# Seven block products for two pairs of gate-and-up chunks a layer, the rest of gate and up in row form, weights in rings

## The chip, the core and the metric

One core of a Trainium2 chip runs the whole program. It has a tensor engine (PE: matrix products and transposes), VectorE (DVE), ScalarE (ACT), GpSimd (POOL) and a queue for transfers on SyncE (SP); every engine works through its own list of instructions in order, and semaphores hold an instruction until what it needs is there. The metric is the device time of the program in microseconds (us).

## What is computed

A trunk of four layers on 256 tokens of width 1024. Each layer has a mixer (layers 0 and 3 banded attention, layer 1 gated linear attention, layer 2 differential attention), a residual with layer norm, then a SwiGLU feed-forward part of hidden width 2816, and again a residual with layer norm:

```python
def swiglu(x, w_gate_up, w_down):
    g, u = jnp.split(x @ w_gate_up, 2, axis=-1)
    return (jax.nn.silu(g) * u) @ w_down

for i in range(DEPTH):
    y = mixer_i(h)
    h = layer_norm(DN_ALPHA * h + y, ln1_g[i], ln1_b[i])
    h = layer_norm(DN_ALPHA * h + swiglu(h, ffn_w_gate_up[i], ffn_w_down[i]), ln2_g[i], ln2_b[i])
```

All inputs are float32. The change touches `x @ w_gate_up` above all: [256 x 1024] by [1024 x 5632] in each layer.

## The kernel before

**Precision.** A float32 value is kept as two float32r parts, high and low (high is the value rounded, low the rest), and a product is made of three matmuls: high with low, high with high, low with high.

**Weights.** They are laid out in DRAM in chunks of 512 columns; a gate-and-up chunk holds 256 columns of the gate and the 256 of the up projection that belong to them, so a layer has 11 such chunks. `w_tiles` (L101) loads two k-tiles of a chunk (512 KB, SP's queue, L109), writes the high part on ACT (L110) and the low part on DVE (L111). There are `RAWB` = 6 buffers for loads and `WB` = 8 for each of the split parts; 4 KB a partition each.

**Two forms of product.** `run_rows` (L141) is row form: tokens on the partitions of the result, 512 weight columns a bank; one step is one k-tile for one half of the tokens, three matmuls (L175 to L177). Half 1 of the tokens runs `lag` steps behind half 0, by default `LAG` = 10, so that a weight tile stays in use for that long. `run_cols` (L182) is column form: the weights stand still, 128 columns at a time, and all 256 tokens stream through, high and low side by side (L196, L197); the four tiles of a chunk stay in use until its last column block. A result in row form has to be transposed to be the next product's stationary input (`split_T`, L219: transposes on PE, the split on ACT L211 and DVE L212); one in column form needs no transpose but an addition of its two halves of the bank (L868, L869).

**Order.** The program is written in one order and the framework's scheduler then fixes each engine's list by that order's priority and by readiness. Work that follows from a finished product is put off by a number of steps (`defer`, `tick`).

**The feed-forward part** (`ffn`, L843): the first two chunks of gate and up in row form (while the second half of the norm is still under way), chunks 2 to 10 in column form, then the down projection in row form, 22 k-tiles by two chunks with the default lag. Row form: ACT takes the silu of the gate (L855), DVE multiplies (L857), and `split_T` turns the result. Scale and shift of the coming norm are loaded by `late_load` (L119) from POOL's queue, each as one [128 x 1024] tile, after POOL has read one column of something just written (L122).

**The norm** (`Norm`, L254) adds the residual on DVE (L276), takes statistics (L287, L300), makes the inverse deviation on POOL (L245, L249), scales and shifts on DVE (L307, L319), and turns the result into the next stage's input `xT`.

**The mixers** run their value (or gate) chunks in row form, the query and key chunks in column form with scores and softmax put in between, and the output projection in row form (`out_proj`).

Of the kernel before, what the change touches and what calls it, by code (L numbers as in the profile page):

```python
# [29 lines left out]
D_SCORES, D_TURN, D_TURN_DIFF, D_VALUES, D_VALUES_DIFF, D_OUT = 4, 7, 6, 3, 2, 6  # L30
D_GATE2, D_GATE3, D_STATE, D_READ, D_GLA_OUT = 3, 8, 2, 4, (6, 5)
D_NORM, D_HIDDEN = 8, 4


@with_exitstack
def trunk_kernel(
# [30 lines left out]
    wp = ctx.enter_context(tc.tile_pool(name="wp", bufs=1))  # L67
    act = ctx.enter_context(tc.tile_pool(name="act", bufs=1))
# [7 lines left out]

    def slab(shape, dtype=F32):
        return act.tile(shape, dtype, tag="slab", bufs=4, name=nm("slab"))

    def k3(shape, dtype=F32):  # L80
        return act.tile(shape, dtype, tag="k3", bufs=5, name=nm("k3"))

    def k2(shape, dtype=F32):
        return act.tile(shape, dtype, tag="k2", bufs=8, name=nm("k2"))

    def k1(shape, dtype=F32):
        return act.tile(shape, dtype, tag="k1", bufs=6, name=nm("k1"))
# [923 lines left out]
```

## Time and profile before

| | us |
|---|---|
| time before, median of 3 runs | 1211.81 (1207.75 to 1213.13) |
| span of the profiled execution | 1209.5 |
| PE busy | 1191.5 (99%) |
| DVE busy | 829.6 (69%) |
| ACT busy | 665.5 (55%) |
| POOL busy | 97.7 (8%) |
| granted TensorE clock, mean of the span | 0.998 of 2.4 GHz |

The profile is of one execution; its span is 2.3 us under the median. PE's share counts the matmuls' modelled ends, which overlap, so the pace is read from the starts of successive matmuls. The gate-and-up stage of layer 0 lies from 123.6 to 248.25 us, its down projection from 248.25 on; the column-form part of layer 1 lies from 441.73 to 541.83.

### The profile page before, as it was taken

The numbers are of one execution on the slowest core, as the hardware profiler recorded it, in microseconds if no ns is written. First come the engines' busy times: TensorE is split into PE (matmuls) and PEld (weight loads), VectorE is DVE, ScalarE is ACT, GpSimd is POOL, SyncE is SP. The second block draws the span as 40 slices with busy tenths as digits, with TensorE's granted clock in tenths as the row PEclk, the third lists the DMA queues.
The fourth block names the chain that finished last, engine by engine and source line by source line (L and its number), as shares of the span: only waits on it lengthen the run. The fifth ranks groups of instructions, "written<-read, shape, count | busy, mean of one in ns | idle before, by whom it ended". The sixth has DMA issues, their size and how long they took to land.

```text
span 1209.5 us, 17080 instructions
## 1 busy us (share of the span) xinstructions
PE 1191.5 (99%) x6224; PEld 993.6 (82%) x6224; DVE 829.6 (69%) x1418; ACT 665.5 (55%) x1169; POOL 97.7 (8%) x188
## 2 busy tenths in 40 slices
PE   7999999999999999999999999999999999999997
PEld 5888888888887888888887778888888888888885
DVE  6687866745656777764667787676466888666644
ACT  6566555643664455663446656556344774665531
POOL 0130000000101000000012110000001200000000
PEclk9999999999999999999999999999999999999999
DMA  9654646556464456555564355665557544655641
GB/s 340 225 189 140 210 173 226 175 176 194 155 229 136 137 195 230 193 184 187 189 226 152 122 168 188 225 198 171 188 185 235 188 126 156 205 208 197 205 143 35
DMA packets 62772, 223.88 MB, mean 185 GB/s; under 512 B 7264, under 2 KB 7776, under 8 KB 62688
## 3 DMA queue, kind: packets, MB, share of 16 engines
q1 hardware_dynamic: 58176, 207.64, 52.1%
q0 software_dynamic: 4512, 15.14, 3.5%
q8 instruction: 49, 0.80, 0.3%
q14 instruction: 35, 0.29, 0.1%
HBM read 221.71 MB, written 1.05 MB: 184 GB/s over the span
## 4 chain that ended last, share of the span: by engine, by line
PE 94%; DVE 2%; ACT 2%; DMA 1%; POOL 0%; issue 0%; SPq 0%; POOLq 0%; DVEq 0%; ACTq 0%
PE mm L196 28%; PE mm L175 15%; PE mm L176 15%; PE mm L197 15%; PE mm L177 15%; PE tp L422 2%; PE tp L224 2%; ACT k L445 1%; PE tp L491 1%; DVE k L430 1%; DMA raw<-in_a_qkv_dram 1%; DVE wl L111 0%; PE tp L512 0%; PE tp L514 0%; PE tp L513 0%
## 5 line engine op out<-in xcount | busy, mean ns | idle before, releaser
L111 DVE TENSOR_TENSOR wl<-raw,wh 128x1024 fp32r<-128x1024 f32 (+1 forms) x394 | 476.0, 1214 | 180.6 <-ACT wh L110 177.7
L196 PE MATMUL mm<-slab,wh 128*128 128x512 f32 x1568 | 555.6, 397 | 0.0
L110 ACT CAST wh<-raw 128x1024 fp32r<-128x1024 f32 (+1 forms) x394 | 406.4, 1047 | 196.7 <-PE mm L177 185.2
L197 PE MATMUL mm<-slab,wl 128*128 128x256 f32 x1568 | 440.8, 281 | 0.0
L196 PEld LDWEIGHTS mm<-slab,wh 128*128 128x128 f32 x1568 | 294.3, 188 | 71.1 <-issue 4.6
L175 PE MATMUL mm<-wl,slab 128*128 128x512 f32 x784 | 311.5, 397 | 7.9 <-DVE wl L111 7.9
L177 PE MATMUL mm<-wh,slab 128*128 128x512 f32 x784 | 307.4, 392 | 0.0
L176 PE MATMUL mm<-wh,slab 128*128 128x512 f32 x784 | 307.2, 392 | 0.0
L197 PEld LDWEIGHTS mm<-slab,wl 128*128 128x128 f32 x1568 | 296.5, 189 | 0.7 <-issue 0.3
L175 PEld LDWEIGHTS mm<-wl,slab 128*128 128x128 f32 x784 | 147.8, 189 | 41.1 <-DVE wl L111 8.5
L177 PEld LDWEIGHTS mm<-wh,slab 128*128 128x128 f32 x784 | 147.6, 188 | 31.7 <-DVE slab L212 0.8
L176 PEld LDWEIGHTS mm<-wh,slab 128*128 128x128 f32 x784 | 147.8, 189 | 30.4 <-issue 1.8
L869 DVE TENSOR_TENSOR k<-mm,k 128x256 f32<-128x256 f32 x144 | 60.6, 421 | 82.9 <-ACT k L868 82.9
L868 ACT COPY k<-mm 128x256 f32<-128x256 f32 x144 | 53.7, 373 | 71.4 <-PE mm L197 71.1
L871 ACT ACTIVATE k<-k 128x256 f32<-128x256 f32 x72 | 29.8, 414 | 46.7 <-DVE k L869 46.7
L245 POOL TENSOR_SCALAR sm<-mv 128x1 f32<-128x1 f32 x16 | 14.1, 883 | 500.4 <-DVE mv L300 500.4
L211 ACT CAST slab<-k 128x256 fp32r<-128x256 f32 (+1 forms) x76 | 31.8, 418 | 40.9 <-DVE k L875 37.4
L212 DVE TENSOR_TENSOR slab<-k,slab 128x256 fp32r<-128x256 f32 (+1 forms) x76 | 33.0, 435 | 23.1 <-ACT slab L211 23.1
L445 ACT ACTIVATE k<-k,nmx 128x128 f32<-128x128 f32 x96 | 42.5, 444 | 8.4 <-DVE nmx L441 8.3
L211 ACT CAST slab<-tp 128x512 fp32r<-128x512 f32 (+1 forms) x56 | 27.1, 495 | 26.6 <-PE tp L224 24.5
L430 DVE CUSTOM_DVE_ANT_0 k<-tp,k 128x128 f32<-128x128 f32 x96 | 28.6, 353 | 10.1 <-PE tp L422 9.0
L212 DVE TENSOR_TENSOR slab<-tp,slab 128x512 fp32r<-128x512 f32 (+1 forms) x56 | 30.6, 569 | 4.6 <-ACT slab L211 4.5
(133 smaller groups left out, 669.5 us busy)
## 6 DMA issues: line engine op xcount, KB each, us to landing
raw<-in_w_gu_dram SPq DMA_DIRECT2D x176, 512.0 KB, 4.4
raw<-in_w_down_dram SPq DMA_DIRECT2D x88, 512.0 KB, 4.2
raw<-in_a_qkv_dram SPq DMA_DIRECT2D x46, 512.0 KB, 4.7
raw<-in_b_in_dram SPq DMA_DIRECT2D x24, 512.0 KB, 3.6
raw<-in_c_qkv_dram SPq DMA_DIRECT2D x24, 512.0 KB, 3.6
raw<-in_a_o_dram SPq DMA_DIRECT2D x16, 512.0 KB, 3.9
k<-in_a_bias_dram POOLq DMA_DIRECT2D x16, 256.0 KB, 4.5
lng<-in_ln_g_dram POOLq DMA_DIRECT2D x8, 512.0 KB, 5.7
```

The lines of the kernel that those rows point to most:

```text
L110: nc.scalar.copy(out=wh[:, k, :], in_=raw[:, k, :])
L111: nc.vector.tensor_tensor(out=wl[:, k, :], in0=raw[:, k, :], in1=wh[:, k, :].bitcast(F32), op=ALU.subtract,)
L175: nc.tensor.matmul(b, xh, wl, start=first, stop=False)
L176: nc.tensor.matmul(b, xh, wh, start=False, stop=False)
L177: nc.tensor.matmul(b, xl, wh, start=False, stop=last)
L196: nc.tensor.matmul(b, wh[:, cs], xk, start=kt == 0, stop=False)
L197: nc.tensor.matmul(b[:, :256], wl[:, cs], xk[:, :256], start=False, stop=kt == NKT - 1)
L211: nc.scalar.copy(out=h, in_=val)
L212: nc.vector.tensor_tensor(out=dst[:, ks, slice(256 + cs.start, 256 + cs.stop)], in0=val, in1=h.bitcast(F32), op=ALU.subtract,)
L445: nc.scalar.activation(pr[:, m, SL[t]], pr[:, m, SL[t]], AF.Exp, bias=nmx[:, t, m : m + 1], accum_out=sm[:, t, m : m + 1],)
L868: nc.scalar.copy(out=lo, in_=b[:, 256:])
L869: nc.vector.tensor_tensor(out=lo, in0=b[:, :256], in1=lo, op=ALU.add)
```

## The change

- **Gate and up in row form.** Chunks 0 and 1 stay as they are. Chunks 2 and 3, and chunks 8 and 9, become two pairs; chunks 4 to 7 and 10 run in row form with a lag of 2 (`PLAIN = (4, 1)`).
- **A pair by seven products.** The input is cut into 2 x 2 blocks (token half by even or odd k-tile), the 1024 columns of the pair into 2 x 2 blocks of weights, b11, b12, b21, b22 (four k-tiles by 512 columns; the host lays each out as one block of 8 KB a partition). `run_seven` makes seven products of 4 steps each instead of eight: of plain blocks and of sums and differences of blocks (Winograd's form of Strassen's scheme). t1 = b12 - b11 and t2 = b22 - t1 are made on DVE, t3 = b22 - b12 and t4 = b21 - t2 on POOL, all written over one of their inputs. Each product's weights are split by `halves` in one piece of 2048 columns. The seven results are added up on DVE, out of PSUM, into the four blocks of the result.
- **Sums of the input.** `blocks_of` puts together the float32 input on POOL (2048 columns a partition), makes the four sums s1 to s4 on POOL (512 columns each) and splits them on ACT and DVE, once a layer.
- **Rings.** Loads come from a ring of 36 KB a partition, split parts from a ring of 56 KB, instead of 24 KB and 64 KB of fixed buffers. A tile takes its room when the tiles that lay there before are released.
- **Pools by stage.** Most activations come from a pool that a mixer or a feed-forward part opens and closes. The hidden values are one tile of 22 k-tiles; the next stage's input has a tile of its own; `k1` has 5 buffers for 6, `k2` 10 for 8, `slab` 3 for 4.
- **Scale and shift** of the norms arrive in halves of 512 columns, four loads for two.

The diff, cut to its core (the lines of `Norm`, of the pools and the comments are left out where they only rename):

```diff
-RAWB = 6  # weight loads under way, 2 k-tiles each
-WB = 8  # split weights on chip, 2 k-tiles each
-LAG = 10  # k-tiles that token half 1 runs behind half 0
+RAW = 36 << 10
+SPLIT = 56 << 10
+LAG = 10
+PLAIN = (4, 1)
...
+    raw_ring = wp.ring(RAW, name="raw")
+    split_ring = wp.ring(SPLIT, name="split")
...
+    def in_stage(fn, *args, **kw):
+        with tc.tile_pool(name=nm("stage"), bufs=1, reuse_waits="tile") as pool:
+            stage.append(pool)
+            fn(*args, **kw)
+            stage.pop()
+    def st(shape, dtype, tag, bufs):
+        return stage[-1].tile(shape, dtype, tag=tag, bufs=bufs, name=nm(tag))
...
-        return act.tile(shape, dtype, tag="slab", bufs=4, name=nm("slab"))
+        return st(shape, dtype, "slab", 3)
-        return act.tile(shape, dtype, tag="k2", bufs=8, name=nm("k2"))
+        return st(shape, dtype, "k2", 10)
...
-        raw = wp.tile([P, 2, 512], F32, tag="raw", bufs=RAWB, name=nm("raw"))
-        wh = wp.tile([P, 2, 512], F32R, tag="wh", bufs=WB, name=nm("wh"))
-        wl = wp.tile([P, 2, 512], F32R, tag="wl", bufs=WB, name=nm("wl"))
+        raw = raw_ring.tile([P, 2, 512], F32, name=nm("raw"))
...
+    def halves(w, n):
+        wh = split_ring.tile([P, n, 512], F32R, name=nm("wh"))
+        wl = split_ring.tile([P, n, 512], F32R, name=nm("wl"))
+        nc.scalar.copy(out=wh, in_=w)
+        nc.vector.tensor_tensor(out=wl, in0=w, in1=wh.bitcast(F32), op=ALU.subtract)
+        return [(wh[:, k, :], wl[:, k, :]) for k in range(n)]
...
+                (to, n, ap.partition_broadcast(P)[:, n * 512 : (n + 1) * 512])
+                for to, ap in ((self.g, g_ap), (self.b, b_ap))
+                for n in range(2)
             ]
...
+    def blocks_of(xT):
+        xf = st([P, NKT, 2 * P], F32, "gb", 1)
+        nc.gpsimd.tensor_tensor(
+            out=xf,
+            in0=xT[:, :, : 2 * P].bitcast(F32),
+            in1=xT[:, :, 2 * P :].bitcast(F32),
+            op=ALU.add,
+        )
+        a11, a12, a21, a22 = (
+            xf[:, k::2, t * P : (t + 1) * P] for t in range(2) for k in range(2)
+        )
+        s1, s2, s3, s4 = f = [st([P, 4, P], F32, "u", 4) for _ in range(4)]
+        nc.gpsimd.tensor_tensor(out=s1, in0=a21, in1=a22, op=ALU.add)
+        nc.gpsimd.tensor_tensor(out=s2, in0=s1, in1=a11, op=ALU.subtract)
+        nc.gpsimd.tensor_tensor(out=s3, in0=a11, in1=a21, op=ALU.subtract)
+        nc.gpsimd.tensor_tensor(out=s4, in0=a12, in1=s2, op=ALU.subtract)
+        x = st([P, 2, 4, 4, P], F32R, "sx", 1)
+        for i in range(4):
+            nc.scalar.copy(out=x[:, 0, i], in_=f[i])
+            nc.vector.tensor_tensor(
+                out=x[:, 1, i], in0=f[i], in1=x[:, 0, i].bitcast(F32), op=ALU.subtract
+            )
+        def plain(k, t):
+            ts = [slice(o + t * P, o + (t + 1) * P) for o in (0, 256)]
+            return lambda p: [xT[:, 2 * p + k, c] for c in ts]
+        def diff(i):
+            return lambda p: [x[:, j, i, p] for j in range(2)]
+        return dict(
+            a11=plain(0, 0), a12=plain(1, 0), a22=plain(1, 1),
+            s1=diff(0), s2=diff(1), s3=diff(2), s4=diff(3),
+        )
+    def run_seven(w, x, done):
+        raw = []
+        for i in range(4):
+            r = raw_ring.tile([P, 4, 512], F32, name=nm("raw"))
+            nc.sync.dma_start(r, w[i].rearrange("p (k n) -> p k n", k=4))
+            raw.append(r)
+        b11, b12, b22, b21 = raw
+        def minus(engine, out, in0, in1):
+            engine.tensor_tensor(out=out, in0=in0, in1=in1, op=ALU.subtract)
+            return out
+        def product(a, w):
+            bk = bank("mm")
+            wts = halves(w, 4)
+            for p in range(4):
+                (xh, xl), (wh, wl) = x[a](p), wts[p]
+                nc.tensor.matmul(bk, xh, wl, start=p == 0, stop=False)
+                nc.tensor.matmul(bk, xh, wh, start=False, stop=False)
+                nc.tensor.matmul(bk, xl, wh, start=False, stop=p == 3)
+                tick(1)
+            return bk
+        def u():
+            return st([P, 512], F32, "u", 4)
+        def plus(out, in0, in1):
+            nc.vector.tensor_tensor(out=out, in0=in0, in1=in1, op=ALU.add)
+        p1 = product("a11", b11)
+        s1, u2, u3, c22 = (u() for _ in range(4))
+        nc.scalar.copy(out=s1, in_=p1)
+        t1 = minus(nc.vector, b11, b12, b11)
+        p5 = product("s1", t1)
+        t3 = minus(nc.gpsimd, b12, b22, b12)
+        t2 = minus(nc.vector, t1, b22, t1)
+        p6 = product("s2", t2)
+        plus(u2, p6, s1)
+        t4 = minus(nc.gpsimd, t2, b21, t2)
+        p7 = product("s3", t3)
+        plus(u3, p7, u2)
+        plus(c22, p5, u3)
+        plus(u2, p5, u2)
+        done(1, 1, c22)
+        p2 = product("a12", b21)
+        plus(s1, p2, s1)
+        done(0, 0, s1)
+        p3 = product("s4", b22)
+        plus(u2, p3, u2)
+        done(0, 1, u2)
+        p4 = product("a22", t4)
+        plus(u3, p4, u3)
+        done(1, 0, u3)
...
+        def turn(c, t, hd):
+            split_T(hd, hid, t, 2 * c, 2)
+            if t == 1 and c >= 5:
+                if not gb:
+                    gb.append(st([P, 4, 512], F32, "gb", 1))
+                norm.load(
+                    hid[:, 2 * c, P : P + 1].bitcast(F32),
+                    lambda sh: gb[0][:, 3 - len(norm.loads)],
+                )
+        run_rows([(plain(c), K8, src, gated(c)) for c in range(2)])
+        x = blocks_of(xT)
+        c = 2
+        for n in PLAIN:
+            run_seven(
+                w[c : c + 2].rearrange("c (i p n) -> (c i) p n", i=2, p=P), x, lambda t, j, y, c=c: gated(c + j)(t, y)
+            )
+            c += 2
+            run_rows([(plain(k), K8, src, gated(k)) for k in range(c, c + n)], lag=2)
+            c += n
...
```

## Rows read from the trace of the kernel before

**Rows 1.** The page's head: span, busy time by engine, end chain by engine.

```profile
span 1209.5 us, 17080 instructions
PE 1191.5 (99%) x6224; PEld 993.6 (82%) x6224; DVE 829.6 (69%) x1418; ACT 665.5 (55%) x1169; POOL 97.7 (8%) x188
...
PE 94%; DVE 2%; ACT 2%; DMA 1%; POOL 0%; issue 0%; SPq 0%; POOLq 0%; DVEq 0%; ACTq 0%
```

**Rows 2.** Windows (stretch and length, busy by engine, clock, DMA): rows, columns, columns.

```profile
123.60:146.28 22.68, 22.68 (x108) 18.74 (x107) 19.11 (x27) 12.15 (x17) 2.00 (x2) 1.00 0.62 199
146.28:248.25 101.97, 101.97 (x580) 88.51 (x578) 68.30 (x106) 60.19 (x107) 3.83 (x7) 1.00 0.58 199
...
441.73:541.83 100.10, 100.10 (x580) 88.25 (x578) 68.20 (x106) 60.55 (x107) 3.56 (x6) 1.00 0.60 204
```

**Rows 3.** Timeline (start, duration, engine, line): row-form steps without and with transposes.

```profile
142.40 0.39 PE L177 MATMUL mm<-wh,slab 128*128 128x512 f32 x1
142.64 0.38 PE L224 MATMUL tp<-ident,k 128*128 128x128 f32 x2
...
143.32 0.40 PE L177 MATMUL mm<-wh,slab 128*128 128x512 f32 x1
...
263.27 0.39 PE L175 MATMUL mm<-wl,slab 128*128 128x512 f32 x1
...
263.95 0.39 PE L175 MATMUL mm<-wl,slab 128*128 128x512 f32 x1
```

**Rows 4.** Groups of instructions by form: count, busy us, mean ns, idle before.

```profile
L111 DVE TENSOR_TENSOR wl<-raw,wh 128x1024 fp32r<-128x1024 f32 x390 | 473.2, 1219 | 179.7 <-ACT wh L110 176.8
L110 ACT CAST wh<-raw 128x1024 fp32r<-128x1024 f32 x390 | 403.9, 1051 | 195.5 <-PE mm L177 185.2 <-PE mm L196 3.1 <-DMA raw<-in_a_qkv_dram 1.8
...
L212 DVE TENSOR_TENSOR slab<-tp,slab 128x256 fp32r<-128x256 f32 x24 | 10.0, 418 | 2.0 <-ACT slab L211 1.9
...
L497 DVE TENSOR_TENSOR k<-tp,k 128x512 fp32r<-128x512 f32 x16 | 11.0, 688 | 3.8 <-ACT k L496 3.7
...
L857 DVE TENSOR_TENSOR k<-k,mm 128x256 f32<-128x256 f32 x16 | 6.6, 414 | 0.6
...
L111 DVE TENSOR_TENSOR wl<-raw,wh 128x512 fp32r<-128x512 f32 x4 | 2.7, 692 | 0.9 <-ACT wh L110 0.9
L110 ACT CAST wh<-raw 128x512 fp32r<-128x512 f32 x4 | 2.5, 618 | 1.1 <-DMA raw<-in_a_qkv_dram 1.1
```

**Rows 5.** Transfers by line: count, KB each, median us from issue to landing.

```profile
raw<-in_w_gu_dram SPq DMA_DIRECT2D x176, 512.0 KB, 4.4
```

**Rows 6.** Timeline of POOL: a fill of one column and of 512.

```profile
0.95 0.10 POOL L98 MEMSET powt<- 128x1 f32 x1
...
83.62 0.53 POOL L637 MEMSET k<- 128x512 f32 x1
```

**Rows 7.** Timeline of POOL and DVE: POOL's one-column reads, alone and beside splits.

```profile
71.73 0.18 POOL L122 COPY lng<-slab 128x1 f32<-128x1 f32 x1 [1.99 <-DVE slab L396]
...
117.66 0.18 POOL L245 TENSOR_SCALAR sm<-mv 128x1 f32<-128x1 f32 x1 [27.44 <-DVE mv L300]
...
127.19 1.17 DVE L111 TENSOR_TENSOR wl<-raw,wh 128x1024 fp32r<-128x1024 f32 x1
127.35 1.05 POOL L245 TENSOR_SCALAR sm<-mv 128x1 f32<-128x1 f32 x1 [8.86 <-DVE mv L300]
...
941.53 2.35 DVE L111 TENSOR_TENSOR wl<-raw,wh 128x1024 fp32r<-128x1024 f32 x2
941.68 2.25 POOL L122 COPY k<-slab 128x1 f32<-128x1 f32 x1 [2.69 <-DVE slab L396]
```

**Rows 8.** Timeline of a down projection: a tile's release and its next split.

```profile
263.04 0.39 PE L177 MATMUL mm<-wh,slab 128*128 128x512 f32 x1
...
263.51 1.05 ACT L110 CAST wh<-raw 128x1024 fp32r<-128x1024 f32 x1 [1.67 <-PE mm L177]
...
264.60 1.22 DVE L111 TENSOR_TENSOR wl<-raw,wh 128x1024 fp32r<-128x1024 f32 x1 [1.50 <-ACT wh L110]
```

More of the change, by code (lines that the diff above doesn't have):

```diff
@@ L101, in w_tiles @@
     def w_tiles(chunk, s, fine=False):
[L104 to L106 removed]
+        raw = raw_ring.tile([P, 2, 512], F32, name=nm("raw"))
+        wh = split_ring.tile([P, 2, 512], F32R, name=nm("wh"))
+        wl = split_ring.tile([P, 2, 512], F32R, name=nm("wl"))
         src = chunk[s].rearrange("p (k n) -> p k n", k=2)
@@ L236, in operand, with input_operand @@
         return slab([P, NKT, 4 * P], F32R)
+    def input_operand():
+        return act.tile([P, NKT, 4 * P], F32R, tag="xT", bufs=1, name=nm("xT"))
     def kt_of(op):
@@ L259, in __init__, with load, add @@
             self.stats = {}
-            self.g = act.tile([P, D], F32, tag="lng", bufs=1, name=nm("lng"))
-            self.b = act.tile([P, D], F32, tag="lnb", bufs=1, name=nm("lnb"))
+            self.scaled = set()
+            self.g, self.b = [None, None], [None, None]
             self.loads = [
-                (self.g, g_ap.partition_broadcast(P)),
-                (self.b, b_ap.partition_broadcast(P)),
-            ]
-        def load(self, seen):
-            if self.loads:
-                late_load(*self.loads.pop(0), seen)
+                (to, n, ap.partition_broadcast(P)[:, n * 512 : (n + 1) * 512])
+                for to, ap in ((self.g, g_ap), (self.b, b_ap))
+                for n in range(2)
+            ]
+        def load(self, seen, tile=None):
+            if not self.loads:
+                return
+            to, n, src = self.loads.pop(0)
+            if n is None:
+                late_load(to, src, seen)
+                return
+            to[n] = (tile or k2)([P, 512])
+            late_load(to[n], src, seen)
+        def add(self, t, n, y):
+            z = self.h[t][:, n * 512 : (n + 1) * 512]
+            if (t, n) in self.scaled:
+                nc.vector.tensor_tensor(out=z, in0=y, in1=z, op=ALU.add)
+                return
+            self.scaled.add((t, n))
+            nc.vector.scalar_tensor_tensor(
+                out=z, in0=z, scalar=ALPHA, in1=y, op0=ALU.mult, op1=ALU.add
+            )
         def part(self, n):
             def done(t, y):
-                z = self.h[t]
-                cs = slice(n * 512, (n + 1) * 512)
-                nc.vector.scalar_tensor_tensor(
-                    out=z[:, cs],
-                    in0=z[:, cs],
-                    scalar=ALPHA,
-                    in1=y,
-                    op0=ALU.mult,
-                    op1=ALU.add,
-                )
+                self.add(t, n, y)
                 if t not in self.stats:
@@ L602, in attention @@
             run_cols(wqkv[g], src, qk_done(g))
-            norm.load(qk_all[:, g, 2, 0:1])
+            for _ in range(2):
+                norm.load(qk_all[:, g, 2, 0:1])
         out_proj(OT, w_o, norm)
@@ L836, in gla @@
         run_cols(w_in[0], src, q_done)
-        norm.load(qT[:, 0, 0:1])
-        norm.load(qT[:, 3, 0:1])
+        for blk in (0, 2, 1, 3):
+            norm.load(qT[:, blk, 0:1])
         run_rows([rows(2, v_done(0)), rows(3, v_done(1)), rows(5, r_done(1))], lag=4)
         out_proj(OT, b_w_o, norm)
+    def blocks_of(xT):
[29 more added lines that the diff above has]
+        )
@@ L843, in ffn, with plain, gated, done @@
     def ffn(xT, layer, norm):
-        hid = []
         w = w_gu[layer]
-        def hid_kt(kt):
-            while len(hid) <= kt // 8:
-                hid.append(operand())
-            return hid[kt // 8][:, kt % 8, :]
-        def row_done(c):
-            def done(t, b):
+        src = kt_of(xT)
+        hid = st([P, NHT, 4 * P], F32R, "hid", 1)
+        gb = []
+        def plain(c):
+            return w[c].rearrange("(s p n) -> s p n", s=NKT // 2, p=P)
+        def gated(c):
+            def done(t, y):
@@ L854, in done @@
                 s = k1([P, 256])
[L855 removed]
+                nc.scalar.activation(s, y[:, :256], AF.Silu)
                 hd = k1([P, 256])
[L857 to L880 removed]
@@ L882, in ffn @@
-        src = kt_of(xT)
-        run_rows([(w[c], K8, src, row_done(c)) for c in range(2)])
-        for c in range(2, FFN // 256):
-            run_cols(w[c], src, col_done(c))
-            if c % 2 == 0:
-                norm.load(hid_kt(2 * c + 1)[:, 0:1].bitcast(F32))
+                nc.vector.tensor_tensor(out=hd, in0=s, in1=y[:, 256:], op=ALU.mult)
+                defer(D_HIDDEN, lambda: turn(c, t, hd))
+            return done
+        def turn(c, t, hd):
[7 more added lines that the diff above has]
+                )
@@ L888, in ffn @@
+        run_rows([(plain(c), K8, src, gated(c)) for c in range(2)])
[4 more added lines that the diff above has]
+                w[c : c + 2].rearrange("c (i p n) -> (c i) p n", i=2, p=P), x, lambda t, j, y, c=c: gated(c + j)(t, y)
+            )
+            c += 2
+            run_rows([(plain(k), K8, src, gated(k)) for k in range(c, c + n)], lag=2)
+            c += n
         run_rows(
             [
-                (w_down[layer, n], range(NHT), hid_kt, norm.part(n))
+                (w_down[layer, n], range(NHT), lambda kt: hid[:, kt, :], norm.part(n))
@@ L913, in trunk_kernel @@
             norm1.loads = [
-                (h[t], x[0, t * P : (t + 1) * P, :]) for t in range(2)
+                (h[t], None, x[0, t * P : (t + 1) * P, :]) for t in range(2)
             ] + norm1.loads
@@ L956, in _layouts @@
     )
-    a["w_gu"] = tiles(a["ffn_w_gate_up"], 11)
+    gu = tiles(a["ffn_w_gate_up"], 11)
+    seven, c = [], 2
+    for n in PLAIN:
+        seven.append(c)
+        c += 2 + n
+    for c in seven:
+        g = gu[:, c : c + 2].reshape(4, 2, 4, 128, 2, 512).transpose(0, 4, 1, 3, 2, 5)
+        g = g.reshape(4, 4, 128, 2048)[:, [0, 1, 3, 2]]
+        gu[:, c : c + 2] = g.reshape(4, 2, 4, 128, 1024)
+    a["w_gu"] = gu.reshape(4, 11, 4 * 128 * 1024)
     a["w_down"] = tiles(a["ffn_w_down"])
```

45 lines of the change are left out of this document (13 added, 32 removed).

## Prediction

> **What bounds the kernel now.** I read the page first: TensorE (PE) is busy for 1191.5 of 1209.5 us and carries 94% of the chain that ended last [rows 1]. So an edit pays only through PE's own work, and every wait that it adds for PE costs in full. The time before is 1211.81 us (median, 1207.75 to 1213.13); the profiled execution's span is 1209.5, so I sum against the span and add 2.3 at the end. About 0.5% (6 us) can be told from no change.
>
> Next the stretches of a gate-and-up stage [rows 2]: two row-form chunks, then nine column-form chunks in 101.97 us (layer 0) and 100.10 us (layer 1), 11.2 us a chunk. PE has no gap there and its clock is 1.00, while VectorE (DVE) is busy for 68 of 102 us and ScalarE (ACT) for 60. The reader should see that DVE has a third to spare on average, and that beside the two row chunks it has less: 19.11 of 22.68 us, since the norm's tail lies there.
>
> Last, the pace of row form [rows 3]. From 263.27 to 263.95 is one k-tile for one token half, 0.68 us for three matmuls, so a chunk of 16 such steps takes 10.88 us. Row form must also transpose the result: two transposes stretch one step from 0.68 to 0.92 (142.40 to 143.32), 0.24 us, twice a chunk. A plain row chunk is 11.36 us, hardly dearer than 11.2 in column form.
>
> **What PE saves.** A pair of chunks in seven products is 7 x 4 steps x 0.68 = 19.0 us, plus 4 x 0.24 for transposes: 20.0, where two column chunks take 22.4. Two pairs save 4.8 a layer; the five other chunks, now in row form, cost 5 x 0.16 = 0.8. That is 4.0 a layer, 16 us in all: 1193.5 if PE never waits.
>
> **What the seven products ask of DVE and ACT.** By [rows 4] a split costs DVE 0.69 us for 512 columns and 1.22 for 1024, so for the 2048 columns of one block 1.22 + 2 x 0.53 = 2.27; a difference on DVE has the same form (two float32 inputs from SBUF), 2.27; the ACT half of a split is 1.05 + 2 x 0.43 = 1.92. Sums out of PSUM are 0.69, the gate 0.41, the split of a transposed result 0.42. A pair in seven products takes DVE 7 splits (15.9), t1 and t2 (4.5), 7 sums (4.8), 4 gates and 4 splits of hidden values (3.3): 28.6 us, against 20.0 of PE. A plain row chunk takes 4 x 1.22 + 2 x 0.83 = 6.5 against 11.4. Over the stage DVE fits; within a pair it is 8.6 us short, and what it can do ahead is limited by the split ring: 56 KB are 7 row tiles of 8 KB or 3.5 products of 16.
>
> The order matters as much. The differences are made in place: t1 overwrites b11, so it waits until b11 is split, and that split needs room in the ring; t2 overwrites t1 likewise. From b11 to the split of t2 there is one chain: split 2.27, t1 2.27, ACT 1.92, split 2.27, t2 2.27, ACT 1.92, split 2.27 = 15.2 us. PE covers p1, p5 and p7 (8.2 us) with products that need less.
>
> **First pair, laid out from the start of the row chunks (0), without GpSimd's reads.** Half 1 runs 10 steps behind, so ring tiles come free late: the third (whose room b11's low part takes) after step 22, at 15.0. The chain would end at 30.2. DVE also owes in that time two gates with their splits and the hidden split of another (2.5), the four splits of the s tiles (2.8) and t3's split (2.27); the two ACT steps cover 3.8 of these 7.6, so the split of t2 ends at 33.9. PE starts p1 at 22.3 and, taking p7 before p6, wants it at 30.4: 3.5 us of waiting. From there DVE needs 3 splits, 6 sums and 3 gates with splits before the last product is fed, at about 46, while PE wants it at 42.5: 3.6 more. b11's 8 KB of the raw ring are held until then, and behind the load that waits for them stand all later weight loads on SP's queue; 4 of 36 KB are spare, one row tile. After 46 a load takes 4.4 us to land [rows 5], then ACT 1.05 and DVE 1.22: 52.7; PE ends the last product and the spare tile at 51.9. Together 8 us.
>
> **Second pair.** Four chunks with lag 2 lie ahead, so the ring turns over one tile per 2.72 us and the chain can begin 13.6 us before p1. The split of t2 is then ready 1.7 us into the pair (wanted at 5.4), the last block's at 16.6 (wanted at 16.8). Only the raw ring bites: loads from 17, a split tile at 23.7 against 22.2: 1.5 us. Waits without GpSimd: 9.5 a layer.
>
> **GpSimd (POOL).** It gets x (2048 columns), four tiles of 512, and t3 and t4 of both pairs: six times 2048 columns a layer, with two SBUF inputs each. Before has no such operation. Its nearest row is a one-stream fill of 512 columns at 0.53 us against 0.10 for one column [rows 6], 0.85 ns a column: 1.8 us if only that counts, 5.2 if two reads and a write take turns. I take two streams, 3.5 us. (The Trainium skill, "GPSIMD Engine Reference", section on performance versus the Vector engine, gives 4.5 us for just this operation, twice DVE's; no row here shows it. An estimate by it, between the two upper prices below, is 20 us more.)
>
> These operations are not beside DVE but in its way. A one-column POOL read takes 0.18 us when DVE is not in an operation with two SBUF inputs, 1.05 when it starts inside one (127.35, beside the split at 127.19), and 2.25 behind two in a row, ending at 943.93 where the second split ends at 943.88 [rows 7]. The rows show POOL waiting for DVE; that DVE waits for a long POOL read is not shown, so the price runs from zero (a rival) to full holding. (The Trainium skill, "SBUF — State Buffer", section "Who interferes with whom", says the pair of ports is an exclusive lock held for the whole instruction, whoever comes first, and that a DVE instruction with two SBUF inputs contends with a GpSimd one that reads SBUF. The rows agree for the one direction.)
>
> With holding, at 3.5 us, in the first pair: x and the s tiles run from about 7 (half 1's first step) for 7 us and DVE's turns of 2 between, to 16, and push the chain's start by one s tile, 0.9; t3 holds up the split of t1 by 1.6 (3.5 less ACT's 1.9); t4 stands before two splits, PE's stock covers some 40% of it: 2.1. Together 4.6. In the second pair t3 fits into DVE's slack, and t4 makes p2 wait 1.5 and the last product 1.9: 3.4. That is 8.0 a layer. At 1.8 us: 0, 0 and 1.1, and 1.9: 3.0. At 5.2: x and s end at 19.4 and push three steps of the chain, 4.0, t3 3.3, t4 3.1, and 6.0: 16.4.
>
> **Moves with one answer.** Scale and shift arrive in halves, four POOL issues for two, now queued behind t3 and t4; their use lies behind the down projection: nothing. Bytes loaded stay the same. Stage pools overlay tiles whose readers are done before the new writers: nothing, unless the gate tiles of the gated layer now wait for the stage before it (one place, under 3 us). The split ring drops from 8 tiles to 7: in the down projection a tile's release (the matmul at 263.04, to 263.43), ACT from 263.51 and DVE from 264.60 end at 265.82 [rows 8], and with one tile less it is wanted at 265.99; it holds by 0.17. In the mixers' 13 column chunks the fourth tile comes later, 0 to 0.5 us each: 0 to 6, I take 2.
>
> **Sum.** A layer: -4.0 + 9.5 + 8.0 = +13.5; four: +54; ring +2; span 1265.5; with the 2.3, **1268**. With POOL at 1.8 and 5.2 us and the ring at 0 and 6: 1246 and 1305.
>
> **Rivals.**
> - *POOL's reads cost DVE nothing* (they slip between its operations). For it: POOL is 8% busy and DVE is not shown waiting. Against: [rows 7]. Then 9.5 - 4.0 a layer: +22, with ring and offset 1236.
> - *Faster: DVE runs ahead far enough, and PE keeps its 16 us.* Place: the ring at the first pair. If the scheduler has b11 to t2 split before p1, by ending the row chunks' hold on the ring early, the 3.5 and 3.6 go, and the rest is short. It decides where the waits fall under 4.0 us a layer. For: DVE's and ACT's means of 0.67 and 0.59 [rows 2]. Against: 28.6 us of DVE in 20.0 of PE. Then 1196, up to 1206.
> - *The raw ring has no spare room* (8 KB blocks that don't fit its end leave 4 KB unused). Each pair then ends with PE waiting a tile longer, 2.7 us x 8: 1290.
>
> **Chances.** Forecast (1246 to 1305) 0.48; POOL free 0.22; faster 0.19; no spare room 0.11. A fifth of the two cases nearest to 1212 falls within 6 us of it. So faster 0.18, same 0.08, slower 0.74. The range leaves out the lower half of the faster case and the top of the last two: 1198 to 1304.
>
> **What would show it.** Right: PE's busy share in the gate-and-up stages falls to about 0.85; PE waits before p5, p6 or p7 and before the first row chunk after a pair, released by DVE's split line; POOL's differences last longer than 3 us, and DVE's 128x2048 splits beside them take 4 us and more, or start late. POOL free: those splits stay at 2.27 whatever POOL does. No spare room: the longest waits are at the row chunk behind each pair, released by ACT's or DVE's split with a DMA ahead of it. Faster: no PE gap over 1 us in a stage, each about 120 us long. Wrong in the first place if a seven-product step is not 0.68 us.

## The result: 1342 us instead of 1212

The changed kernel takes 1342.2 us (median; 1341.65 to 1344.08) beside 1212.5 us of the kernel before on the same chip: a ratio of 1.109, 95% interval [1.106, 1.111]. It is slower, as forecast, but by 130 us where the prediction had 56, and above its range of 1198 to 1304.

The head of the page after, as in [rows 1]: span, busy time by engine, chain by engine.

```profile
span 1341.0 us, 15752 instructions
PE 1229.7 (92%) x5696; PEld 980.0 (73%) x5696; DVE 951.5 (71%) x1354; ACT 662.6 (49%) x1041; POOL 239.2 (18%) x256
...
PE 10%; DVE 3%; issue 1%; ACT 1%; POOL 1%; DMA 0%; POOLq 0%; DVEq 0%; ACTq 0%
```

PE has 528 fewer matmuls than before and yet 38 us more of busy time, where the prediction has 16 less. The count alone does not show that: 432 of the 528 go because row form has fewer, longer matmuls (experiment 2 has 5792). But the other 96, which the seven products save, should have made PE's work shorter, and it became longer. PE also has about 101 us of gaps, which before added up to 9. What PE waited for (us in total, times, longest):

```profile
PE mm L941 <- DVE wl L142: 45.0, 12, 5.7
PE tp L250 <- DVE k L993: 28.1, 25, 2.5
PE mm L201 <- DVE wl L129: 23.1, 11, 6.8
```

L941 is a block product, L142 the split of a block. All three lines name VectorE (DVE); no DMA is among them, except behind 6.8 of the 23.1 us, which is the wait for the very first weights of the program. The groups by form (count, busy us, mean ns, idle before), answering [rows 4, 6]: DVE's part of the block splits, the differences on POOL and on DVE, the first sum of the input on POOL:

```profile
L142 DVE TENSOR_TENSOR wl<-raw,wh 128x2048 fp32r<-128x2048 f32 x56 | 167.7, 2995 | 25.8 <-ACT wh L141 23.0 <-issue 2.5 <-PE mm L943 0.3
L933 POOL TENSOR_TENSOR raw<-raw,raw 128x2048 f32<-128x2048 f32 x16 | 73.3, 4584 | 142.4 <-DVE wl L142 75.3 <-DVE raw L933 67.0
L933 DVE TENSOR_TENSOR raw<-raw,raw 128x2048 f32<-128x2048 f32 x16 | 36.4, 2277 | 0.0
L887 POOL TENSOR_TENSOR gb<-xT 128x2048 f32<-128x2048 f32 x4 | 18.3, 4585 | 17.3 <-DVE xT L238 17.3
```

A difference takes 2.28 us on DVE (2.27 forecast) and 4.58 us on GpSimd (POOL; 3.5 forecast). A DVE split takes 3.0 us in the mean instead of 2.28. The timeline shows which ones are long, answering [rows 7]:

```profile
151.63 4.56 POOL L933 TENSOR_TENSOR raw<-raw,raw 128x2048 f32<-128x2048 f32 x1 [7.23 <-DVE raw L933]
153.58 4.75 DVE L142 TENSOR_TENSOR wl<-raw,wh 128x2048 fp32r<-128x2048 f32 x1 [1.71 <-ACT wh L141]
...
240.22 4.63 POOL L933 TENSOR_TENSOR raw<-raw,raw 128x2048 f32<-128x2048 f32 x1 [6.04 <-DVE wl L142]
240.71 6.29 DVE L142 TENSOR_TENSOR wl<-raw,wh 128x2048 fp32r<-128x2048 f32 x1
247.26 2.28 DVE L142 TENSOR_TENSOR wl<-raw,wh 128x2048 fp32r<-128x2048 f32 x1
```

All 12 splits that begin inside a POOL difference end 2.15 us after POOL does (here 158.33 against 156.19, 247.00 against 244.85), wherever they began; the next, with POOL quiet, takes 2.28.

Layer 0's first and second pair, and the first pair in slices (columns as in [rows 2]: PE's busy time first, the granted clock as the third number from the end):

```profile
150.60:184.90 34.30, 24.14 (x89) 18.67 (x89) 25.68 (x21) 16.55 (x16) 9.10 (x2) 0.80 0.36 126
236.40:259.90 23.50, 20.35 (x89) 15.40 (x88) 21.54 (x18) 13.82 (x15) 8.03 (x5) 1.00 0.51 181
...
152.00:158.00 6.00, 1.77 (x9) 1.11 (x7) 4.42 (x1) 3.60 (x3) 4.18 (x1) 0.87 0.00 0
158.00:164.00 6.00, 5.29 (x12) 3.80 (x12) 5.29 (x5) 3.34 (x4) 0.00 (x0) 0.56 0.00 0
164.00:170.00 6.00, 0.77 (x2) 0.71 (x3) 4.36 (x2) 2.75 (x2) 0.84 (x1) 0.73 0.49 175
170.00:176.00 6.00, 6.00 (x20) 4.70 (x20) 1.73 (x2) 1.91 (x1) 3.71 (x1) 0.70 0.19 42
```

In the first slice PE works for 1.77 of 6 us; in the second it is busy and the granted clock is 0.56, near the lower level (1.2 of 2.4 GHz). The matmuls of p5 there, answering [rows 3]:

```profile
158.39 0.79 PE L941 MATMUL mm<-wl,sx 128*128 128x512 f32 x1 [4.61 <-DVE wl L142]
...
159.40 0.63 PE L943 MATMUL mm<-wh,sx 128*128 128x512 f32 x1
159.83 0.63 PE L941 MATMUL mm<-wl,sx 128*128 128x512 f32 x1
160.26 0.63 PE L942 MATMUL mm<-wh,sx 128*128 128x512 f32 x1
```

0.427 us from start to start, 1.28 for a step of three, where the prediction has 0.68. In the whole trace 133 row-form matmuls follow each other at 0.40 to 0.46 us (8 before). The mean clock is 0.964 (0.998 before).

### The profile page after: what moved, and what is told of

Read it like the earlier page. It is cut to its first block, busy times and chain, and to the rows that moved or that the text cites. A ratio compares the mean times of both kernels' runs of the same rounds, so it can differ in the third digit from the quotient of the medians.

```text
span 1341.0 us, 15752 instructions
## 1 busy us (share of the span) xinstructions
PE 1229.7 (92%) x5696; PEld 980.0 (73%) x5696; DVE 951.5 (71%) x1354; ACT 662.6 (49%) x1041; POOL 239.2 (18%) x256
## 5 line engine op out<-in xcount | busy, mean ns | idle before, releaser
L201 PE MATMUL mm<-wl,xT 128*128 128x512 f32 x624 | 254.6, 410 | 24.6 <-DVE wl L129 23.1
L202 PE MATMUL mm<-wh,xT 128*128 128x512 f32 x624 | 249.4, 400 | 0.0
L203 PE MATMUL mm<-wh,xT 128*128 128x512 f32 x624 | 247.4, 401 | 0.0
L142 DVE TENSOR_TENSOR wl<-raw,wh 128x2048 fp32r<-128x2048 f32 x56 | 167.7, 2995 | 25.8 <-ACT wh L141 23.0
L201 PEld LDWEIGHTS mm<-wl,xT 128*128 128x128 f32 x624 | 120.6, 193 | 55.5 <-DVE wl L129 28.1
L222 PE MATMUL mm<-xT,wh 128*128 128x512 f32 x416 | 151.9, 403 | 0.0
L141 ACT CAST wh<-raw 128x2048 fp32r<-128x2048 f32 x56 | 106.5, 1909 | 78.9 <-PE mm L941 34.5
L201 PE MATMUL mm<-wl,hid 128*128 128x512 f32 x352 | 140.8, 400 | 0.0
L203 PE MATMUL mm<-wh,hid 128*128 128x512 f32 x352 | 139.7, 397 | 0.0
L202 PE MATMUL mm<-wh,hid 128*128 128x512 f32 x352 | 139.5, 396 | 0.0
L203 PEld LDWEIGHTS mm<-wh,xT 128*128 128x128 f32 x624 | 120.0, 192 | 26.6 <-DVE xT L238 0.4
L202 PEld LDWEIGHTS mm<-wh,xT 128*128 128x128 f32 x624 | 121.0, 194 | 24.6 <-issue 1.3
L223 PE MATMUL mm<-xT,wl 128*128 128x256 f32 x416 | 117.8, 283 | 0.0
L941 PE MATMUL mm<-wl,sx 128*128 128x512 f32 x128 | 59.0, 461 | 45.0 <-DVE wl L142 45.0
```

The source lines that it names most:

```text
L141: nc.scalar.copy(out=wh, in_=w)
L142: nc.vector.tensor_tensor(out=wl, in0=w, in1=wh.bitcast(F32), op=ALU.subtract)
L201: nc.tensor.matmul(b, xh, wl, start=first, stop=False)
L202: nc.tensor.matmul(b, xh, wh, start=False, stop=False)
L203: nc.tensor.matmul(b, xl, wh, start=False, stop=last)
L222: nc.tensor.matmul(b, wh[:, cs], xk, start=kt == 0, stop=False)
```

## Experiments

Each kernel starts from the changed one unless it says otherwise; medians in us, ratios to the kernel before on the same chip.

**1. All differences on DVE.**

```diff
-        t3 = minus(nc.gpsimd, b12, b22, b12)
+        t3 = minus(nc.vector, b12, b22, b12)
```

and likewise t4 and the five sums of the input.

> All differences on VectorE, nothing of the pairs on GpSimd. Theory 1 (a GpSimd read of on-chip memory holds VectorE for about as long as it runs): a layer loses six operations of 4.58 us that hold VectorE (27.5 us) and gets six more VectorE operations of about 2.3 us (13.8 us), and t3 and t4 are ready earlier; with a PE idle of 101 us in the changed kernel the time falls by 25 to 55 us, to 1285 to 1317 us, and every 2048-column weight split on VectorE is near 2.3 us instead of a mean of 3.0. Theory 2 (GpSimd runs beside VectorE, the waits come from the order alone): VectorE has 13.8 us a layer more work on the path of the pairs and the time rises by up to 30 us, to 1340 to 1370 us.

Measured: 1294.6, ratio 1.068 [1.065, 1.071], 47.6 less, with more work on the engine that PE waits for. The splits:

```profile
L142 DVE TENSOR_TENSOR wl<-raw,wh 128x2048 fp32r<-128x2048 f32 x56 | 127.0, 2283 | 11.1 <-ACT wh L141 9.9 <-PE mm L943 1.2
```

All 56 are back at 2.28 us. Theory 1 holds; 59 us are left over the form without pairs (next). In layer 0's first pair DVE is now busy for 29.23 of 30.03 us:

```profile
143.97:174.00 30.03, 24.38 (x97) 19.14 (x96) 29.23 (x22) 15.90 (x14) 0.00 (x0) 0.89 0.38 132
```

**2. No pairs.** `PLAIN = ()`, chunks 2 to 10 in row form, no sums of the input.

> Gate and up projections all in row form, token half 1 two k-tiles behind half 0, no pairs and no block sums; the rings, the buffers per stage and the rest of the change stay. Theory 1 (the pairs lose the time): 9 chunks of row form cost 9 x 0.16 = 1.4 us a layer more than column form, and the slower stretches outside the gate and up projections (5 us before the pairs, 4 to 10 us after them) partly stay, so 1215 to 1245 us. Theory 2 (the rings and the row form themselves cost it, the pairs are near their arithmetic): the time stays above 1290 us.

Measured: 1235.5, ratio 1.019 [1.017, 1.022]. Theory 1: the pairs cost 107 us, the rest of the change 22.

**3. Constants in place of t3 and t4.**

```diff
+            if engine is nc.gpsimd:
+                for v in (1.0, 2.0):
+                    nc.gpsimd.memset(out, v)
+                nc.gpsimd.memset(out[:, 0:2, :], 0.01)
...
+                return out
```

> t3 and t4 of each pair are not computed: GpSimd fills their tiles with constants for about the same 4.6 us and reads nothing from on-chip memory; their weight splits stay. This leaves the differences b12 - b22 and t2 - b21 out. Theory 1 (it is the reading that holds VectorE): weight splits beside the fills take 2.3 us instead of 3.4 to 6.3, and the time falls by 20 to 40 us to 1300 to 1320 us. Theory 2 (t3 and t4 are late because GpSimd is slow, whatever it does): the fills are as late as the differences, VectorE splits may be shorter, but the time stays within 10 us of 1342 us.

Measured: 1306.8, 35 less, ratio 1.078 [1.075, 1.081]. By form:

```profile
L142 DVE TENSOR_TENSOR wl<-raw,wh 128x2048 fp32r<-128x2048 f32 x56 | 131.9, 2363 | 22.8 <-ACT wh L141 22.8
...
L935 POOL MEMSET raw<- 128x2048 f32 x32 | 58.0, 1812 | 125.4 <-DVE raw L938 67.1 <-DVE wl L142 57.4
```

POOL is as long at work at the same places (2 x 1.81 + 0.96 = 4.6 us), but only writes, and the splits beside it are short: 52 of the 56 take 2.28 to 2.29 us, and the other four, 3.36 us, run beside the sums of the input, for which POOL still reads. It is the reading that holds DVE. That this kernel is still 12 us behind experiment 1 fits the x sums, which stay on POOL here, and the late fills; the two are not told apart.

**4. Work for PE in the waits.** In the first pair of each layer 20 and 24 unread matmuls ahead of p5 and p6.

> Before the products p5 and p6 of the first pair of each layer 20 and 24 matmuls that nothing reads are added, so that TensorE has work while it would wait for t1 and t2. Theory 1 (the idle time ahead of p5 and p6 is what the half-speed granted clock follows, 0.56 to 0.73 in that stretch): p5 and p6 run at 0.227 us a matmul again instead of 0.427, which is 24 to 48 x 0.2 us = 5 to 10 us a layer, and the time falls by 15 to 30 us. Theory 2 (the granted clock falls for another reason, or the added matmuls only move the waits): no change, or up to 15 us slower.

Measured: 1333.6, 8.6 less, ratio 1.101 [1.097, 1.105]. The same stretch:

```profile
152.00:158.00 6.00, 6.00 (x29) 4.82 (x27) 4.46 (x1) 3.52 (x3) 4.21 (x1) 1.00 0.00 0
158.00:164.00 6.00, 5.88 (x26) 4.58 (x25) 6.00 (x5) 5.53 (x5) 0.00 (x0) 1.00 0.00 0
164.00:170.00 6.00, 6.00 (x28) 4.90 (x27) 3.69 (x3) 0.65 (x1) 4.62 (x1) 1.00 0.48 175
170.00:176.00 6.00, 6.00 (x28) 4.87 (x27) 6.00 (x4) 2.97 (x2) 1.98 (x1) 1.00 0.51 170
```

The clock stays at 1.00, and adding 176 matmuls makes the kernel faster. So the idle time brings the clock down, and that costs something of its own. The gain is under the 15 to 30 expected: the half-paced matmuls fall from 133 to 69, 64 x 0.2 = 13 us, and what the added ones run over is paid for.

**5 and 6. The order of the products**, p1, p2, p3, p5, p7, p6, p4: three products that need no difference come first. Once with POOL, once with DVE alone.

```diff
         t3 = minus(nc.gpsimd, b12, b22, b12)
+        p2 = product("a12", b21)
...
+        p3 = product("s4", b22)
+        nc.scalar.copy(out=s3, in_=p3)
+        p5 = product("s1", t1)
         t2 = minus(nc.vector, t1, b22, t1)
+        p7 = product("s3", t3)
         p6 = product("s2", t2)
```

> The seven products in another order: p1, p2, p3, p5, p7, p6, p4 instead of p1, p5, p6, p7, p2, p3, p4, so that three products stand ahead of the first difference and the splits come in the order of the products; t3 and t4 stay on GpSimd; two more tiles of sums. Theory 1 (a pair waits where a difference and its split are late, the order decides it): the 12 waits ahead of products, 45.0 us in all, fall to under 15 us, and with the clock behind them the time falls by 30 to 50 us, to 1290 to 1312 us. Theory 2 (VectorE's work in the pair is simply longer than the 20.0 us of products, the order only moves the wait): within 15 us of 1342 us.

> The same order with all differences and sums on VectorE. Theory 1 (holding and order add up): 1255 to 1275 us, 20 to 40 us under the 1294.6 us of the old order with VectorE alone. Theory 2 (seven splits and four differences are 11 x 2.28 = 25 us of VectorE for 20.0 us of products, so VectorE is the bound in any order): within 12 us of 1294.6 us.

Measured: 1361.9, ratio 1.124 [1.122, 1.126], and 1308.2, ratio 1.080 [1.078, 1.082]: 20 and 14 slower than in the old order. Theory 1 falls in both, and both also lie beyond the ranges of theory 2 (15 and 12 us). One window over the first pair with POOL, one with DVE alone:

```profile
143.70:180.00 36.30, 27.56 (x110) 20.94 (x109) 33.02 (x22) 17.26 (x20) 10.60 (x4) 0.91 0.18 64
...
143.70:173.40 29.70, 21.95 (x90) 17.15 (x88) 29.15 (x22) 15.43 (x16) 0.00 (x0) 0.94 0.32 118
```

DVE (fourth number) is busy, or held by POOL, for 33.02 of 36.30 us, and without POOL for 29.15 of 29.70. This order does not make the full engine faster, and it puts t1 and t3 ahead of the split that p2 needs, which may be why it is slower. A third order was not tried.

**7. t3 and t4 left out**, on the kernel of experiment 1.

> Differences on VectorE as in the 1294.6 us run, and t3 and t4 left out (b12 and t2 are split as they stand), so a pair has 9 VectorE operations of 2.28 us instead of 11. Theory 1 (VectorE is the bound of a pair once GpSimd is out of it): 8 x 2 x 2.28 = 36 us of VectorE less, 25 to 40 us less time, 1255 to 1270 us. Theory 2 (the chain of difference, split and product is what is late, t3 and t4 stand off it): under 12 us less.

Measured: 1280.5, ratio 1.057 [1.054, 1.059], 14 less than experiment 1: between the theories. In this trace DVE and ACT wait for each other around p5 and p6 (3.5 and 2.0 us in layer 0), which fits that, with less DVE work, the chain of difference, ACT's copy and split sets the first pair, as it did in the prediction; no run takes that chain alone.

**8. One pair a layer, later**, DVE alone: chunks 7 and 8, the sums of the input five chunks ahead.

> One pair a layer instead of two, chunks 7 and 8, with all differences and sums on VectorE, the sums of the input made five chunks earlier; chunks 0 to 6, 9 and 10 in row form. Theory 1 (the first pair of a layer carries the loss, because sums, splits and differences meet in one stretch, and a pair with slack ahead of it waits 4 us and saves 2.4 us): 1235.5 + 4 x 1.6 = about 1242 us, between 1235 and 1250 us. Theory 2 (each pair costs its VectorE surplus, wherever it stands): half of the 59 us between 1294.6 and 1235.5 us, 1265 us. Theory 3 (with slack ahead the waits hide): 1226 us.

Measured: 1252.6, ratio 1.034 [1.032, 1.036], between theories 1 and 2, nearer to 1 but above its range. Layer 0, the pair with what follows, then its last parts:

```profile
206.00:230.00 24.00, 20.28 (x86) 15.40 (x85) 23.55 (x27) 16.62 (x21) 2.03 (x6) 0.94 0.63 222
224.00:230.00 6.00, 2.87 (x10) 1.77 (x10) 6.00 (x10) 5.13 (x9) 1.14 (x4) 0.74 0.59 194
230.00:236.00 6.00, 6.00 (x20) 4.78 (x19) 4.51 (x5) 0.61 (x1) 0.53 (x1) 0.69 0.76 244
```

Inside the pair PE waits 0.6 us at most; DVE runs full for 24 us, and its debt comes due behind the pair: PE works 2.9 of 6 us, then runs at a clock of 0.69. A layer loses 17.1 / 4 = 4.3 us to its pair where 2 x 11.36 - 20.0 = 2.7 should have been saved. PE's waits in the stage are 3.7 to 4.0 us a layer, as theory 1 had them; what it left out is the clock behind them. So the surplus of DVE costs in this place too. Two pairs lose 59.1 / 4 = 14.8 a layer, so the first place costs more.

**9 and 10. What the change loses without pairs.** From experiment 2: the rings as large as the buffers before (24 and 64 KB), and the gated layer's constants in memory of their own.

> The form without pairs (1235.5 us) with the rings as large as the buffers of the kernel before: 24 KB for loads, 64 KB for splits, so 8 splits of 2 k-tiles instead of 7. Theory 1 (the down projection lost 2.4 us a layer to the seventh split): the down projection takes 59.8 us again instead of 62.4 to 63.3 and the time falls by 8 to 12 us, to about 1225 us. Theory 2 (8 splits do not matter, as the prediction's margin of 0.17 us said): 1235 us or, with less room for loads, more.

> The form without pairs with the three 2 KB constants of the gated layer (mask, two gate weights) in memory of their own instead of the layer's stage memory; loads ring 28 KB instead of 36 KB. Theory 1 (their fills and loads now wait until the hidden tile of the layer before is read, from 318.7 us on, and TensorE waits 1.7 us for the last load and then runs 10 us at the lower granted clock): that stretch takes 7 to 9 us less, 1226 to 1229 us. Theory 2 (the loads were not what the stretch waited for): 1235 us.

Measured: 1229.0, ratio 1.014 [1.013, 1.016], and 1229.3, ratio 1.015 [1.013, 1.016]. The timeline of experiment 2, POOL's first fill and last load of the constants, PE's wait for that load and matmuls behind it, and a window there:

```profile
318.66 0.52 POOL L653 MEMSET k<- 128x512 f32 x1
...
322.72 0.48 POOL L689 DMA_DIRECT2D k<-in_b_b_g_dram  x1
...
324.57 1.53 PE L727 MATMUL tp<-k,k 65*128 65x512 f32 x2 [1.70 <-DMA k<-in_b_b_g_dram]
...
330.22 0.63 PE L201 MATMUL mm<-wl,xT 128*128 128x512 f32 x1
330.64 0.63 PE L202 MATMUL mm<-wh,xT 128*128 128x512 f32 x1
...
330.00:336.00 6.00, 6.00 (x17) 4.37 (x17) 1.98 (x3) 3.60 (x6) 0.00 (x0) 0.50 0.00 0
```

The fills and loads stand where the stage before ends; in the kernel before they were long done. The wait is 1.7 us, but matmuls at 0.42 us follow, at a granted clock of 0.50. With memory of their own the fills of the constants are out of this stretch and 6.2 us come back, a little less than theory 1 has (7 to 9). But the ring sizes of before gain as much, and not where I had said: the down projection takes 63.2 us with 7 splits and with 8, so theory 1 of that run falls and the prediction's "holds by 0.17" stands. It is the same stretch that shrinks, although the fills and loads stand where they stood; the same wait there:

```profile
323.12 1.10 PE L727 MATMUL tp<-k,k 65*128 65x512 f32 x2 [0.23 <-DMA k<-in_b_b_g_dram]
```

The clock stays at 1.00 there in both kernels. What is shown is that this stretch costs some 6 us where PE waits for the constants and the clock falls. That only their place brings this about is not shown: both kernels also have a smaller ring for loads (24 and 28 KB for 36), which was not tried by itself.

**11 to 15. Matmuls of stage tiles.** The timeline of a down projection in the kernel after, two starts that lie three matmuls apart:

```profile
1290.13 0.39 PE L201 MATMUL mm<-wl,hid 128*128 128x512 f32 x1
...
1290.83 0.39 PE L201 MATMUL mm<-wl,hid 128*128 128x512 f32 x1
```

The same in the kernel before:

```profile
1160.15 0.39 PE L175 MATMUL mm<-wl,slab 128*128 128x512 f32 x1
...
1160.83 0.39 PE L175 MATMUL mm<-wl,slab 128*128 128x512 f32 x1
```

0.70 against 0.68 us, and so in the median for the 1824 matmuls whose stationary tile lies in stage memory (hid, the hidden values; slab, the input of an output projection; sx, the sums of the input); those of xT keep 0.68. What differs is where the tile starts in memory, so an unused tile was put ahead of it, here one of 928 bytes a partition:

```diff
     xT = input_operand()
+    pad = act.tile([P, 232], F32, tag="pad", name="pad")
+    nc.gpsimd.memset(pad, 0.0)
```

The runs: with 32 bytes; with 32 bytes on experiment 10; in the kernel before with 32 bytes ahead of everything; with 928 bytes; and with 2976 bytes on experiment 10.

> The changed kernel with one unused tile of 32 bytes a partition ahead of the stage memory, so that every stage tile starts 32 bytes further on: at 32 beyond a multiple of 64 bytes, like the rings, xT and every tile of the kernel before, where it stood on a multiple of 64. In the traces so far matmuls whose stationary operand lies in stage memory (hid, sx, slab) start 0.235 us apart, all others 0.2267 us. Theory 1 (it is the start of the stationary tile against that of the moving one): 1056 + 384 + 384 = 1824 matmuls x 0.0083 us = 15 us less where nothing else is late; 10 to 16 us less, 1326 to 1332 us, and hid's matmuls at 0.2267 us. Theory 2 (it is what kind of tile it is, or what runs beside it): no change, 0.235 us stays.

> The form without pairs with the gated layer's constants apart (1229.3 us) and the same 32 bytes. Theory 1 (start of the tile): 1440 matmuls of hid and slab x 0.0083 us = 12 us less, about 1217 us, which leaves 5 us over the kernel before: that is the row form. Theory 2: 1229 us.

> The kernel before with 32 unused bytes ahead of all large tiles: weights and operands both start on multiples of 64 bytes instead of both 32 beyond. Theory 1a (what counts is that moving and stationary tile start alike): no change, 0.2267 us a matmul, 1212 us. Theory 1b (a stationary tile on a multiple of 64 is slow by itself): about 2350 row matmuls and 3100 column matmuls x 0.0083 us = up to 45 us slower.

> The changed kernel with 928 unused bytes a partition ahead of the stage memory instead of 32: all stage tiles then start at the same remainder modulo 4096 bytes (672) as the split weights, as xT does here and as every operand did in the kernel before; with 32 bytes they agreed modulo 128 bytes and hid's matmuls stayed at 0.2333 us. Theory 1 (the step depends on how the two tiles start against each other, modulo more than 128 bytes): hid, slab and sx at 0.2267 us, 1824 matmuls x 0.0083 us = 15 us, so 1326 to 1333 us. Theory 2 (something else of the stage tiles): 0.233 to 0.235 us, 1342 us.

> The form without pairs, the gated layer's constants in memory of their own, stage tiles at remainder 672 as well (2976 unused bytes). Theory 1: 1440 matmuls x 0.0083 us = 12 us less than 1229.3 us, about 1217 us; what is left over the kernel before, 5 us, is the row form. Theory 2: 1229 us.

Measured: 1342.6 and 1229.8 with 32 bytes, no change (steps 0.70 us still): the guess modulo 64 falls. 1208.6 for the kernel before with both kinds of tile shifted alike, ratio 0.998 [0.997, 0.999]. With the remainder modulo 4096 bytes that the weights have, 1339.3, ratio 1.105 [1.102, 1.108], and 1225.0, ratio 1.011 [1.009, 1.013]; the timeline of the down projection with 928 bytes:

```profile
1290.25 0.39 PE L201 MATMUL mm<-wl,hid 128*128 128x512 f32 x1
...
1290.93 0.39 PE L201 MATMUL mm<-wl,hid 128*128 128x512 f32 x1
```

0.68 again. **16.** The counter-proof, 128 bytes between weights and operands of the kernel before:

> The kernel before with 128 unused bytes between the weights and the operands, so that operand tiles start 128 bytes further on against the split weights. Theory 1 (relative start of the two tiles): row matmuls (2352) at 0.233 us instead of 0.2267 us, and the column form's as well if it is symmetric, 15 to 40 us slower. Theory 2: 1212 us, 0.2267 us.

Measured: 1222.7, ratio 1.009 [1.007, 1.011]; the timeline of its last down projection:

```profile
1170.11 0.40 PE L175 MATMUL mm<-wl,slab 128*128 128x512 f32 x1
...
1170.81 0.39 PE L175 MATMUL mm<-wl,slab 128*128 128x512 f32 x1
```

0.70 us here; the column form keeps its pace. So the relative start of the two tiles sets this pace, shown both ways. The pace came as expected, the times did not. It is worth 4.3 us where PE is the bound (1229.3 to 1225.0; 12 were expected): the down projections take 5.5 us less, but the gate-and-up stages 1.9 more, and why is open. In the kernel before it is 10.7 (15 to 40 expected). In the kernel with pairs the 2.9 us (15 expected) lie within the intervals.

## Why the prediction was too low, step by step

Three runs split the loss as the prediction's own sum does. Expected shares: row form 9 x 0.16 x 4 = 6 and rings 2; pairs without POOL 54 - 32 - 6 = 16; POOL 8.0 x 4 = 32.

| part | expected | measured |
|---|---|---|
| row form, rings, stage memory (experiment 2 over before) | +8 | +22.3 |
| pairs, all on DVE (experiment 1 over 2) | +16 | +59.1 |
| POOL (changed kernel over experiment 1) | +32 | +47.6 |

The second row holds more than the share beside it: experiment 1 has t3, t4 and the sums of the input on DVE, some 14 us a layer that the 16 does not price, and the third row is less by what that costs. Nearest to the share is experiment 7, where t3 and t4 are left out: 45.1 over experiment 2. By PE's time, the 74 us by which the sum was too low are 38 of slower work of PE, 18 of longer gaps (22 a layer for 17.5) and 14 of the first row; some 4 are not assigned.

- *POOL holds DVE*: right, with the mechanism as told (experiments 1 and 3). The rival "POOL's reads cost DVE nothing" falls. The size was off in one factor, 4.58 us for 3.5; between its own prices at 3.5 and 5.2 us (8.0 and 16.4 a layer) 4.58 gives 13.3, and 11.9 was measured, less the DVE work that experiment 1 has instead. The Trainium skill ("GPSIMD Engine Reference", performance versus the Vector engine) has 4.5 us for an addition of this size, and the trace agrees: 4.58. The Trainium skill ("SBUF — State Buffer", "Who interferes with whom") has a DVE instruction with two SBUF inputs contend with POOL's reads and not with its mere writes: the trace agrees, with splits of 2.28 us alone and 4.75 and 6.29 beside reads, and with 2.28 to 2.29 beside the fills of experiment 3.
- *Waits without POOL, 9.5 us a layer*: nearly right as waits. PE's gaps in the gate-and-up stages of experiment 1 are 10.0 to 16.1 a layer, 12.4 in the mean, with the longest ahead of p5 in place of p6; in experiment 7, nearer to what the term prices, 10.1. In the changed kernel they are 22 where the prediction has 17.5, and PE's busy share in these stages is 0.86, its sign of being right (0.85).
- *PE's pace, 0.68 us a step*: this is the step that failed, the one that the prediction named as the one to go wrong in the first place. It priced gaps and took the clock for 1.00 throughout, as [rows 2] showed it, where PE had no gap; the slow matmuls behind a gap it put at nothing. PE's busy time in experiment 1 is 6 us over that of experiment 2 although 96 matmuls (21.8 us) are gone: 28 us, 7 a layer. 93 more half-paced matmuls (108 against 15) explain 19 of them, the starts of the sx tiles 3; the rest is not told apart. In experiment 7 it is 20 us, in the changed kernel 38.5, by the same count. That idle time brings the clock down is shown by experiment 4, for the first pair and for 13 us of it. 12.4 gaps and 7.0 pace, less the 5.4 that two pairs save over row form, make 14.0 a layer, 56 of the 59 measured.
- *Order*: the prediction took p7 ahead of p6. PE keeps the written order p6, p7, while the splits of t3 (in b12's place) and b21 come ahead of that of t2: p6 waits 5.55 us in layer 0. t2 is made by 160.87, but ACT, which splits first, stands idle for 2.66 us until PE is through with p5, then splits two blocks, and the DVE split that p6 waits for starts right behind the second, at 166.79:

```profile
158.59 2.28 DVE L933 TENSOR_TENSOR raw<-raw,raw 128x2048 f32<-128x2048 f32 x1
...
163.06 3.70 ACT L141 CAST wh<-raw 128x2048 fp32r<-128x2048 f32 x2 [2.66 <-PE mm L941]
```

So room in the split ring has a part in this wait; with pairs no other ring size was tried. The other order did not help, and with it DVE is full (experiments 5 and 6).
- *Raw ring*: PE's waits at the first row chunk behind a pair are 1.3 us at most, not among the longest. The rival "no spare room" falls.
- *Moves with one answer*: "under 3 us" for the gated layer's constants, which the sum has at nothing, was some 6 (experiments 9 and 10), again because PE's clock dropped behind a short wait. The place of the stage tiles had no term: 4.3. The seventh split ring tile held. The row form costs what was forecast: the four gate-and-up stages of experiment 2 take 504.4 us against 498.6 before, 5.8 for 6. Of the 22.3 then 11.8 are left. Between the spans of experiment 15 and before, 14.6 us, 7.7 lie in the gate-and-up stages, 3.4 in the down projections and 3.5 in the mixers and the rest; what the part beyond the row form comes from is open.
- *Faster*: its condition, waits under 4 us a layer, came nowhere near with two pairs; a single pair with room ahead has waits of 3.7 to 4.0 us and still loses 4.3 a layer.

None of the variants is faster than the kernel before. Experiment 13, that kernel with 32 unused bytes, is 0.2% below it, too little to count as faster.

## What to carry over

Before you trade matmuls for differences, add up what the block asks of the engine that prepares its operands: 28.6 us of VectorE per 20 us of TensorE, 33 with t3 and t4, did not pay here in either of the two orders or the two places that were tried. A difference moved to GpSimd is not off VectorE's path: while it read on-chip memory for 4.6 us, VectorE's splits beside it took up to 6.29 us in place of 2.28. And price a wait of TensorE twice, once as idle time and once as slow matmuls behind it.

## Not expected of the hardware

- After a gap of 4.6 us at p5 the granted clock is 0.56 and matmuls run at 0.427 instead of 0.227 us; filling this gap and the one at p6 in each layer, with 176 useless matmuls in all, makes the kernel 8.6 us faster.
- How moving and stationary tile start against each other in on-chip memory changes the pace of row-form matmuls by 3%: 0.70 against 0.68 us for three. Equal remainders modulo 4096 bytes were fast; differences of 96 and 128 bytes modulo 256 were slow. Which modulus counts was not tried further.
- With both shifted alike by 32 bytes the kernel before took 0.2% less; why is open.
